# Seven block products in place of eight: the first layer's in-projection of a two-layer decoder trunk, heads 1 to 7

## The chip, the core and the metric

One core of one Trainium2 chip runs the whole program. The metric is the device time of one execution in microseconds (us), lower is better. The core has five engines with an instruction stream each: TensorE (PE) multiplies matrices and transposes, VectorE (DVE) and ScalarE (ACT) work element by element, GpSimd (POOL) does a few small operations and issues those DMAs that add to what is at their destination, and SyncE (SP) issues most of the others. Each works through its own stream in order and waits on semaphores for the others. Matrix products end in PSUM, eight banks of 128 partitions x 512 float32 each; everything else lives in SBUF or, outside the core, in HBM.

## The reference

Two residual layers on 512 tokens of width 2048. Only the first concerns us: RMSNorm, one input projection to queries, keys, values and gate, differential attention with 8 heads, and an output projection.

```python
proj = h @ w_in                                   # (512, 2048) @ (2048, 8192)
q, k, v, gate = jnp.split(proj, 4, axis=-1)
q = q.reshape(B, T, DA_HEADS, 2, DA_HEAD_DIM)     # 8 heads, two halves of 128
v = v.reshape(B, T, DA_HEADS, DA_VALUE_DIM)       # 256 a head
q = apply_rope(rms_norm(q, q_gain), cos, sin)
k = apply_rope(rms_norm(k, k_gain), cos, sin)
...
s = jnp.einsum('bqhcd,bkhcd->bhcqk', qj, k) * scale
p = jax.nn.softmax(jnp.where(mask, s, neg), axis=-1)
a = p[:, :, 0] - lam * p[:, :, 1]
o = jnp.einsum('bhqk,bkhd->bqhd', a, vf)
...
o = rms_norm(o, subln_w) * (1.0 - lambda_init)
return (o * jax.nn.silu(gate)) @ w_out
```

The second layer is RWKV-7 time mixing with projections of its own; the change leaves it alone.

## The kernel before

Every large product is made of three matmuls: each float32 operand is split into a high and a low part, and `mm3` (L127) adds high x high, high x low and low x high. The weights come from HBM in float32: `load_w` (L73) issues the DMA on SP into a tile `wraw` of two K tiles (K is the contracted dimension, 2048 = 16 tiles of 128 rows), and `split_w` (L98) makes `wh` on ACT (L115) and `wl` on DVE (L116). There are three buffers of `wraw` and four each of `wh` and `wl`. The normalised input, transposed, stays in SBUF for the whole layer as `hH` and `hL`, 16 pairs of tiles of 128 rows x 512 tokens.

Per head the layer runs two units, `unit_tok` (L194): first queries and keys, then values and gate. A unit has 512 columns and 512 tokens; it goes through the 16 K tiles, and for each multiplies the four token tiles into the four banks `pp`: 16 x 4 x 3 = 192 matmuls. After the first unit `head_qk` (L297) copies the banks out, applies the rotary tables and the norms; `turn_qk` (L342) transposes the result into `qkT` and `qkL`. After the second, `head_vg` (L353) makes `V`, `VL` and the gate `G` straight from the banks.

The attention of the head before runs inside these units. A `Chain` (L135) is a list of steps; `tick` (L179) counts projection matmuls and puts in the next step when its gap has passed, 40 matmuls for a round of `attention` (L373): scores and softmax of a block of 128 queries, the transposes of `a`, the weighing of `V`, the transposes of `y`. So PE always has projection matmuls between two steps of attention. Two PSUM banks hold scores, one the transposes (tag `pb`), one the weighing. The scheduler writes each engine's stream; work under `high_priority` moves ahead of its place in the program (splits by 2000, steps of a chain by 5000).

The last head's attention runs inside the output projection, with a gap of 21. The output projection already makes half of its columns with seven products (`seven`, L530), on 12 of its 16 K tiles, with sums of weight blocks made by DMAs that add (`add_w`, L524).

Of the kernel before, what the change touches and what calls it, by code (L numbers as in the profile page):

```python
# [296 lines left out]
def head_qk(g, h, qk):  # L297

    nc, w = g.nc, g.work
    sq = g.small.tile([P, NT, 2], F32, name="sq", tag="sq")  # L300
    ss = g.small.tile([P, NT, 4], F32, name="ss", tag="ss")
    rr = g.small.tile([P, NT, 4], F32, name="rr", tag="rr")
    t1s = []
    for t in range(NT):
        t1s.append(w.tile([P, 512], F32, name="t1", tag="t1", bufs=4))
        with g.tc.high_priority(offset=AHEAD):
            nc.scalar.copy(t1s[t][:], qk[t][:])
    for t in range(NT):
        squares = w.tile([P, 512], F32, name="squares", tag="junk", bufs=2)
        t1 = t1s[t]  # L310
        nc.scalar.activation(squares[:], t1[:], AF.Square, scale=g.rstd0[:, t : t + 1])
        t2 = w.tile([P, 512], F32, name="t2", tag="t2", bufs=1)
        t1v = t1[:].rearrange("p (a b c) -> p a b c", a=2, b=2)
        t2v = t2[:].rearrange("p (a b c) -> p a b c", a=2, b=2)

        def tab(x, lo, hi):
            return x[:, t, :, None, lo:hi].to_broadcast([P, 2, 2, hi - lo])

        nc.vector.tensor_mul(t2v[:, :, :, 0:64], t1v[:, :, :, 64:128], tab(g.S, 0, 64))
        nc.vector.tensor_mul(t2v[:, :, :, 64:128], t1v[:, :, :, 0:64], tab(g.S, 64, 128))  # L320
        nc.vector.reduce_sum(ss[:, t, :], squares[:].rearrange("p (c d) -> p c d", c=4), AX.X)
        nc.vector.tensor_mul(t1v, t1v, tab(g.C, 0, P))
        nc.vector.tensor_add(t1[:], t1[:], t2[:])
# [1311 lines left out]
```

## Time and profile before

| | |
|---|---|
| three runs | 2149.81, 2147.76, 2150.05 us; median 2149.81 |
| the profiled execution | 2147.86 us, of which the span of the core 2146.2 us |
| granted TensorE clock | 1.00 of full speed |
| first layer, heads 2 to 6 | 98.6 to 99.0 us each |
| last attention and output projection | about 770 to 1040 us of the span |
| HBM read and written in the span | 207.5 and 16.0 MB |

How to read the lines: a row by stretch gives start and end, the stretch in us, and then the busy time of PE, PE's weight loads, DVE, ACT and POOL, each with its number of instructions, then the granted clock, the DMA engines' busy share and GB/s. A group row gives line, engine, operation, output <- inputs, shapes and count, then busy us and mean ns of one, and after the second bar the idle time ahead of them and what ended it. A timeline row gives start and length in us. Matmuls overlap, so a matmul's length (0.39 us) is more than the time from one start to the next. A DMA row ends in KB each and the median us from issue to landing.

### The profile page before, as it was taken

The page shows a single profiled execution, that of the slowest core. Times are in us where ns is not written, and L with a number is a line of the kernel's source. Part 1 is how long each engine was busy: PE and PEld are TensorE (multiplying, and loading weights), DVE is VectorE, ACT ScalarE, POOL GpSimd, SP SyncE. Part 2 cuts the span into 40 slices and gives each one's busy share as a digit, 9 for nine tenths or more (in the row PEclk, how much of TensorE's full clock was granted, in tenths as well). Part 3 has the DMA queues.
Part 4 walks back from the last instruction along what each step waited for, and adds up shares of the span by engine and source line. Part 5 has one row for each costly group of instructions (what it writes and reads, how often), then busy time and mean ns, then how long its engine had stood idle before and what let it go on. Part 6 is the DMA issues. An engine that isn't in the chain of part 4 may idle for free.

```text
span 2146.2 us, 34955 instructions
## 1 busy us (share of the span) xinstructions
PE 2125.3 (99%) x12260; PEld 1753.2 (82%) x12260; DVE 1547.9 (72%) x4137; ACT 1125.5 (52%) x2587; POOL 339.5 (16%) x614
## 2 busy tenths in 40 slices
PE   9999999999999999999999999999999999999999
PEld 8888888888888887887878888888888888877887
DVE  5665647464656668457789888888888888887645
ACT  6444434343444455445666666666666666666333
POOL 0000000000000000011033233333333223343011
PEclk9999999999999999999999999999999999999999
DMA  6223232322223365672222323222223232345566
GB/s 197 91 82 105 80 99 79 101 97 89 90 87 99 99 196 172 190 152 85 79 69 72 85 77 83 81 77 77 77 77 86 68 81 77 86 125 162 194 168 118
DMA packets 258625, 225.77 MB, mean 105 GB/s; under 512 B 12337, under 2 KB 220481, under 8 KB 258449
## 3 DMA queue, kind: packets, MB, share of 16 engines
q1 hardware_dynamic: 239504, 188.03, 29.5%
q0 software_dynamic: 10080, 19.50, 4.6%
q10 hardware_dynamic: 8864, 16.01, 2.0%
q8 instruction: 96, 1.57, 0.3%
q14 instruction: 81, 0.66, 0.1%
HBM read 207.50 MB, written 15.99 MB: 104 GB/s over the span
## 4 chain that ended last, share of the span: by engine, by line
PE 91%; DVE 5%; ACT 2%; issue 1%; DMA 1%; POOL 0%; ACTq 0%; DVEq 0%; POOLq 0%
PE pp L129 71%; PE pt L129 5%; PE gp L1137 1%; PE o L129 1%; PE sc L129 1%; PE sm L1356 1%; PE sm L1378 1%; PE lora L129 1%; PE sm L1369 1%; DMA yr<-yd 1%; PE Y L1402 1%; DVE wl L116 1%; PE pt L1197 1%; PE pt L346 1%; PE z L129 1%
## 5 line engine op out<-in xcount | busy, mean ns | idle before, releaser
L116 DVE TENSOR_TENSOR wl<-wraw,wh 128x512 fp32r<-128x512 f32 (+1 forms) x636 | 440.4, 694 | 341.3 <-ACT wh L115 335.4
L115 ACT CAST wh<-wraw 128x512 fp32r<-128x512 f32 (+1 forms) x636 | 392.7, 619 | 490.3 <-PE pp L129 387.6
L129 PE MATMUL pp<-wh,hH 128*128 128x512 f32 x1268 | 500.2, 394 | 0.6 <-DVE prmin_rw_mu_dram L234 0.6
L129 PE MATMUL pp<-wh,hL 128*128 128x512 f32 x1268 | 498.1, 393 | 0.0
L129 PE MATMUL pp<-wl,hH 128*128 128x512 f32 x1268 | 497.4, 392 | 0.0
L129 PE MATMUL pp<-hH,wh 128*128 128x512 f32 x1024 | 417.6, 408 | 0.0
L129 PE MATMUL pp<-hL,wh 128*128 128x512 f32 x1024 | 413.2, 404 | 0.0
L129 PE MATMUL pp<-hH,wl 128*128 128x512 f32 x1024 | 413.1, 403 | 0.0
L129 PEld LDWEIGHTS pp<-wh,hL 128*128 128x128 f32 x1268 | 238.4, 188 | 48.6 <-DVE hL L908 0.2
L129 PEld LDWEIGHTS pp<-wh,hH 128*128 128x128 f32 x1268 | 238.4, 188 | 48.3 <-issue 1.3
L129 PEld LDWEIGHTS pp<-wl,hH 128*128 128x128 f32 x1268 | 238.5, 188 | 47.1
L129 PEld LDWEIGHTS pp<-hH,wh 128*128 128x128 f32 x1024 | 193.1, 189 | 38.1 <-issue 1.1
L129 PEld LDWEIGHTS pp<-hH,wl 128*128 128x128 f32 x1024 | 193.4, 189 | 33.3
L129 PEld LDWEIGHTS pp<-hL,wh 128*128 128x128 f32 x1024 | 193.3, 189 | 32.1
L1364 POOL COPY SA<-VS 64x64 f32<-64x64 f32 x224 | 75.2, 336 | 524.8 <-DVE VS L1382 466.2
L1230 DVE SCALAR_TENSOR_TENSOR tmpl<-LT,n,Tm 128x60 f32<-128x60 f32 (+24 forms) x496 | 135.8, 274 | 13.3
L500 POOL DMA_DIRECT2D frow<-yd x12 | 8.9, 742 | 794.6 <-DVE rs_t L67 675.7
L1233 DVE TENSOR_TENSOR Tm<-Tm,tmpl 128x60 f32<-128x60 f32 (+24 forms) x496 | 106.2, 214 | 13.6
L1359 ACT COPY rhs<-sm 64x64 f32<-64x64 f32 x256 | 52.5, 205 | 64.0 <-PE sm L1356 61.1
L1371 ACT COPY VS<-sm 64x64 f32<-64x64 f32 x256 | 52.8, 206 | 55.8 <-PE sm L1369 49.5
L1382 DVE SCALAR_TENSOR_TENSOR VS<-sm,gam,Sg 64x64 f32<-64x64 f32 x192 | 53.9, 281 | 21.7 <-PE sm L1378 16.9
L1356 PEld LDWEIGHTS sm<-VS,G 128*128 128x128 f32 x256 | 47.4, 188 | 17.3 <-PE pp L129 4.3
(339 smaller groups left out, 3284.2 us busy)
## 6 DMA issues: line engine op xcount, KB each, us to landing
wraw<-in_rw_w_in_dram SPq DMA_DIRECT2D x128, 512.0 KB, 4.0
wraw<-in_da_w_in_dram SPq DMA_DIRECT2D x254, 256.0 KB, 3.0
wraw<-in_da_w_out_dram SPq DMA_DIRECT2D x26, 512.0 KB, 4.3
wraw<-in_rw_w_out_dram SPq DMA_DIRECT2D x26, 512.0 KB, 4.3
yr<-yd SPq DMA_DIRECT2D x28, 256.0 KB, 3.4
frow<-yd POOLq DMA_DIRECT2D x12, 512.0 KB, 6.9
xq<-in_x_dram SPq DMA_DIRECT2D x16, 256.0 KB, 5.4
xd<-xq ACTq DMA_DIRECT2D x16, 256.0 KB, 4.1
```

Source lines behind the costliest of these rows:

```text
L115: nc.scalar.copy(hi[:], raw[:, k : k + n])
L116: nc.vector.tensor_sub(lo[:], raw[:, k : k + n], hi[:].bitcast(F32))
L129: m = nc.tensor.matmul(out, a, b, start=s, stop=e, skip_group_check=skip)
L346: nc.tensor.transpose(pt[:, c * P : (c + 1) * P], t1s[t][:, c * P : (c + 1) * P], g.ident[:])
L1137: m = nc.tensor.matmul(gp[h][:, i * P : (i + 1) * P], BK[r_, c0 + i, :, :], p.AR[r_, c0 + i, :, :], start=True, stop=True)
L1230: st = nc.vector.scalar_tensor_tensor(tt, LT[:, i : i + 1, i + 1 :].to_broadcast([P, s, n]), n2[:, i : i + 1], Tm[:, 0:s, i : i + 1].to_br ...
L1233: nc.vector.tensor_add(Tm[:, 0:s, i + 1 :], Tm[:, 0:s, i + 1 :], tt)
L1356: nc.tensor.matmul(sm[:, 0:P], both(p.G[:, c, 0]), both(VS[:, c]), start=True, stop=True)
L1359: rc = nc.scalar.copy(rhs[r_, :], sm[r_, h * C : h * C + C])
L1364: nc.gpsimd.tensor_copy(p.SA[r_, c - 1, :], VS[r_, c, h, :])
L1371: vc = nc.scalar.copy(VS[r_, c, h, :], sm[r_, P : P + C])
L1382: g.state = nc.vector.scalar_tensor_tensor(VS[r_, c + 1, h, :], s_, p.gam[r_, c : c + 1], Sg[r_, :], ALU.mult, ALU.add)
```

## The change

For heads 1 to 7, ten of the sixteen K tiles are taken as two halves of five, the 512 columns of `w_in` stand as two halves of 512 (queries and keys; values and gate), and the tokens as two halves of 256. On these 2 x 2 blocks the product is made with seven block products instead of eight, in the Strassen-Winograd form. The other six K tiles are multiplied as before. What is new in the text:

- `Seven.forms` makes, inside head 0's second unit, the sums of input blocks S1, S2, S4 (their own tiles), and S3 in place of one block of `hH` and `hL`.
- `Seven.head` replaces both units of a head. The four banks are two pairs, B and A, which take turns; results that are needed later go to four SBUF tiles `u` (`U`, `W`) by copies on ACT and sums on DVE (`take`, L646).
- Sums of weight blocks are made in the tile `T` (five K tiles) and, for S1, in `wraw`: a plain DMA of SP, then DMAs of POOL that add. `prime` starts the next head's `T`.
- A split (`Seven.split`) serves two token tiles, 6 matmuls, in the products and 12 in the plain part.
- Room for these tiles comes from the attention, whose `qkT`, `qkL`, `p0`, `p1`, `at`, `al`, `y` have one buffer instead of two; `a` is written over `p0`. The round of attention has a new order and a gap of 37. The squares of `rope` are now four instructions with the sum read from the accumulator, in place of one and a reduction.
- In the output projection the homes of `xq`, of the sums and of loads move to other tiles.

```diff
-            qk = unit_tok(g, g.hH, g.hL, qk_cols(aps, h), 512) if h else qk0
-            t1s, sq = head_qk(g, h, qk)
-            qkT = head_qkT(g)
...
-            vg = unit_tok(g, g.hH, g.hL, [(win, 2 * D + h * 256, 256), (win, 3 * D + h * 256, 256)], 512)
...
+        vg = unit_tok(g, g.hH, g.hL, [(win, 2 * D, 256), (win, 3 * D, 256)], 512, more=u.forms, late=False)
...
+        for h in range(1, NH):
+            Chain(g, attention(g, h - 1, *before, 37), 28)
+            before = u.head(h)
...
+KP = 5
+GROUPS = ((0, 2), (2, 2), (4, 1))
+class Seven:
...
+    def fetch(self, raw, k0, half, h, add=False):
+        n = raw.shape[1]
+        src = self.win[k0 * P : (k0 + n) * P, 2 * half : 2 * half + 2, h, :].rearrange("(k p) f c -> p k f c", p=P)
+        for f in range(2):
+            o, i = raw[:, :, f * 256 : f * 256 + 256], src[:, :, f, :]
+            if add:
+                self.g.nc.gpsimd.dma_start(out=o, in_=i, accum_op=ALU.add)
+            else:
+                self.g.nc.sync.dma_start(out=o, in_=i)
...
+    def mm(self, out, lhs, w, first, end):
+        for t in range(2):
+            mm3(self.g.nc, out[t][:], *lhs(t), w[0][:], w[1][:], first, end, self.g, True)
+    def product(self, out, lhs, h, raw, first, groups=GROUPS, then=None, end=True):
+        for k, n in groups:
+            for i, w in enumerate(self.split(raw(k, n))):
+                kk = k + i
+                self.mm(out, lhs(kk), w, first and kk == 0, end and kk == KP - 1)
+            if then:
+                then(k, n)
+    def plain(self, half, h, outs):
+        for k in range(2 * KP, KT, 2):
+            ws = self.split(self.raw(2, k, half, h))
+            for x, out, first, end in outs:
+                for i, w in enumerate(ws):
+                    self.mm(out, self.rows(k + i, x), w, first and k + i == 2 * KP, end and k + i == KT - 1)
...
+    def head(self, h):
+        q = QK(g)
+        self.product(B, lambda k: self.rows(k, 1), h, tile_of, True, then=more(0, 0))
+        self.product(A, top, h, lambda k, n: self.raw(n, k, 0, h), True)
+        self.copy(W, B)
+        self.product(B, low, h, lambda k, n: self.raw(n, KP + k, 0, h), True, end=False)
+        self.copy(q.t1s[:2], A)
+        self.product(A, lambda k: self.form("S2", k), h, tile_of, False, then=more(KP, 0), end=False)
+        self.copy(U, A)
+        self.plain(0, h, ((0, B, False, True), (1, A, False, False)))
+        self.take(q.t1s[:2], q.t1s[:2], B)
+        self.product(A, lambda k: self.rows(KP + k, 1), h, tile_of, False)
+        if h + 1 < NH:
+            self.prime(h + 1)
+        for t in range(2):
+            rope(g, q, t)
+        self.take(q.t1s[2:], A, W)
+        self.product(B, lambda k: self.form("S1", k), h, lambda k, n: self.raw(n, k, 0, h, (k, 1)), True)
+        for t in range(2, NT):
+            rope(g, q, t)
+        norm_qk(g, q)
+        qkT = head_qkT(g)
+        Chain(g, keys(g, q, qkT, 18), 20)
+        last = lambda k, n: self.raw(n, KP + k, 1, h)
+        s4 = lambda k: self.form("S4", k)
+        self.take(U, B, U, ALU.subtract)
+        self.product(A, s4, h, last, True, GROUPS[:1])
+        self.plain(1, h, ((0, A, False, False), (1, B, True, True)))
+        self.take(W, U, W, ALU.subtract)
+        self.product(A, s4, h, last, False, GROUPS[1:])
+        vg = VG(g)
+        for c in list(g.chains):
+            c.finish(g)
+        self.take(W, W, B)
+        self.take(U, U, A)
+        with g.tc.high_priority(offset=AHEAD if h == NH - 1 else 0):
+            for t, x in ((2, W[0]), (3, W[1]), (0, U[0]), (1, U[1])):
+                vg.convert(g, t, x)
...
     for i in range(NT + 3):
+        if i > 2:
+            turn_y(i - 3)
+        if i == NT + 2:
+            break
+        if 1 < i:
+            weigh(i - 2)
         if 0 < i <= NT:
             turn(i - 1)
-        if i == NT + 2:
-            turn_y(i - 3)
-            break
         yield 8
-        if i > 1:
-            weigh(i - 2)
-        if i > 2:
-            turn_y(i - 3)
         if i < NT:
             scores(i)
         yield gap - 8
```

Three places in the streams. First DVE, early in a head's work on values and gate, where the rotary steps (`t`, `t1`, `t2`) and the norm's small steps (`rs_i`, `rs_t`) of the same head stand among the splits `wl`. Before, in the middle of head 2's second unit, the two splits of a load stand among the same steps, and nothing there reads `pp`:

```order
L64 TENSOR_SCALAR rs_i_2733<-rs_i_2733 128x1
L324 TENSOR_SCALAR ss_2610<-ss_2610 128x16
L322 TENSOR_TENSOR t1_2616<-t1_2616,ropeC_642 128x512
L67 TENSOR_TENSOR rs_t_2734<-rs_i_2733 128x1
L116 TENSOR_TENSOR wl_2800<-wraw_2796,wh_2799 128x512
L68 SCALAR_TENSOR_TENSOR rs_t_2734<-rs_t_2734,so_2729 128x1
L116 TENSOR_TENSOR wl_2804<-wraw_2796,wh_2803 128x512
L70 SCALAR_TENSOR_TENSOR rs_i_2733<-rs_t_2734,rs_i_2733 128x1
L323 TENSOR_TENSOR t1_2616<-t1_2616,t2_2638 128x512
```

Now, in head 2, around the end of the product with S1 (into banks 1242 and 1243; `u` are the four SBUF tiles):

```order
L70 SCALAR_TENSOR_TENSOR ro_2948<-rs_t_2950,rs_i_2949 128x1
L607 TENSOR_TENSOR wl_3133<-wraw_3125,wh_3132 128x512
L454 TENSOR_TENSOR ro_2948<-ro_2948,r_2784 128x1
L324 TENSOR_TENSOR t1_2326<-t1_2326,t2_3079 128x512
L455 SCALAR_TENSOR_TENSOR y_2944<-o_2931,ro_2948,G_2288 128x256
L646 TENSOR_TENSOR u_1246<-pp_1242,u_1246 128x512
L646 TENSOR_TENSOR u_1247<-pp_1243,u_1247 128x512
L646 TENSOR_TENSOR u_1248<-u_1246,u_1248 128x512
L646 TENSOR_TENSOR u_1249<-u_1247,u_1249 128x512
L607 TENSOR_TENSOR wl_3152<-wraw_3148,wh_3151 128x512
L607 TENSOR_TENSOR wl_3156<-wraw_3148,wh_3155 128x512
L607 TENSOR_TENSOR wl_3194<-wraw_3190,wh_3193 128x512
```

Four sums that read the product's banks have come in between the last split of S4's first group (`wl_3133`) and the first split of the plain part (`wl_3152`).

Second PE, in the round of attention with three blocks in flight. Before (head 2's first unit): the transposes of `a` into `pt`, eight projection matmuls, then the weighing into `o`:

```order
L129 MATMUL pp_2147<-wh_2481,hH_462 128x512
L410 MATMUL pt_2501<-ident_79,a_2456 128x128 x3
L129 MATMUL pp_2147<-wl_2482,hH_462 128x512
L129 MATMUL pp_2147<-wh_2481,hL_463 128x512
L129 MATMUL pp_2148<-wh_2481,hH_462 128x512
L129 MATMUL pp_2148<-wl_2482,hH_462 128x512
L129 MATMUL pp_2148<-wh_2481,hL_463 128x512
L129 MATMUL pp_2149<-wh_2481,hH_462 128x512
L129 MATMUL pp_2149<-wl_2482,hH_462 128x512
L129 MATMUL pp_2149<-wh_2481,hL_463 128x512
L129 MATMUL o_2517<-V_2115,at_2385 128x256
```

Now, at the same round (`a` lies in `p0`):

```order
L460 MATMUL yt_2707<-ident_79,y_2588 128x128 x2
L129 MATMUL o_2711<-V_2286,at_2611 128x256
L129 MATMUL o_2711<-VL_2287,at_2611 128x256
L129 MATMUL o_2711<-V_2286,al_2612 128x256
L129 MATMUL o_2711<-V_2286,at_2611 128x256
L129 MATMUL o_2711<-VL_2287,at_2611 128x256
L129 MATMUL o_2711<-V_2286,al_2612 128x256
L436 MATMUL pt_2738<-ident_79,p0_2642 128x128 x3
```

The transposes of `y` and the weighing have moved ahead of the transposes of `a`, without projection matmuls between; `yt` and `pt` are the same bank.

Third POOL, between the constants and the output projection. Before, nothing stands there:

```order
L223 DMA prow_1132<-in_rw_mu_dram 64x128
L971 DMA mut_1134<-in_rw_mu_dram 2x96
L500 DMA frow_8587<-yd_75 128x2x512 x2
L500 DMA frow_8655<-yd_75 128x2x512 x2
L500 DMA frow_8746<-yd_75 128x2x512 x2
L526 DMA ropeC_642<-in_da_w_out_dram 128x2x512
```

Now, one head's share of the adding DMAs: into `wraw` for S1, into the next head's `T`, and twice more into `T` in that head:

```order
L575 DMA wraw_3009<-in_da_w_in_dram 128x2x256 x2
L575 DMA wraw_3034<-in_da_w_in_dram 128x2x256 x2
L575 DMA wraw_3059<-in_da_w_in_dram 128x256 x2
L575 DMA T_715<-in_da_w_in_dram 128x2x256 x4
L575 DMA T_715<-in_da_w_in_dram 128x256 x2
L575 DMA T_715<-in_da_w_in_dram 128x2x256 x4
L575 DMA T_715<-in_da_w_in_dram 128x256 x2
L575 DMA T_715<-in_da_w_in_dram 128x2x256 x4
L575 DMA T_715<-in_da_w_in_dram 128x256 x2
```

These are 24 DMAs that were not there, in a stream that was empty in this part of the program.

More of the change, by code (lines that the diff above doesn't have):

```diff
@@ L294, in lambda_full @@
     nc.vector.tensor_scalar(g.neglam[:], g.neglam[:], LAMBDA_INIT, None, ALU.subtract)
[L297 to L323, printed above, removed]
@@ new lines, with __init__, rope, tab @@
+class QK:
+    def __init__(self, g):
+        self.t1s = [g.work.tile([P, 512], F32, name="t1", tag="t1", bufs=4) for _ in range(NT)]
+        self.sq = g.small.tile([P, NT, 2], F32, name="sq", tag="sq")
+        self.ss = g.small.tile([P, NT, 4], F32, name="ss", tag="ss", bufs=2)
+        self.rr = g.small.tile([P, NT, 4], F32, name="rr", tag="rr", bufs=2)
+def rope(g, q, t):
+    nc, t1 = g.nc, q.t1s[t]
+    t2 = g.work.tile([P, 512], F32, name="t2", tag="t2", bufs=1)
+    for c in range(4):
+        cs = slice(c * P, (c + 1) * P)
+        nc.scalar.activation(t2[:, cs], t1[:, cs], AF.Square, scale=g.rstd0[:, t : t + 1],
+                             accum_out=q.ss[:, t, c : c + 1])
+    t1v = t1[:].rearrange("p (a b c) -> p a b c", a=2, b=2)
+    t2v = t2[:].rearrange("p (a b c) -> p a b c", a=2, b=2)
+    def tab(x, lo, hi):
+        return x[:, t, :, None, lo:hi].to_broadcast([P, 2, 2, hi - lo])
+    nc.vector.tensor_mul(t2v[:, :, :, 0:64], t1v[:, :, :, 64:128], tab(g.S, 0, 64))
+    nc.vector.tensor_mul(t2v[:, :, :, 64:128], t1v[:, :, :, 0:64], tab(g.S, 64, 128))
+    nc.vector.tensor_mul(t1v, t1v, tab(g.C, 0, P))
+    nc.vector.tensor_add(t1[:], t1[:], t2[:])
@@ L377, in attention @@
+def attention(g, h, qkT, qkL, sq, vg, gap, rows=None):
+    nc, w = g.nc, g.work
+    V, VL, G = vg.V, vg.VL, vg.G
     yT = w.tile([P, 2, T], F32, name="yTh", tag="yTh", bufs=1)
@@ L513, in sum_forms @@
         else:
-            at = [pool.tile([P, n, 256], F32R, name="f" + nm, tag=t, bufs=m)[:] for pool, t, m in tags]
+            at = [x[0].tile([P, n, 256], F32R, name="f" + nm, tag=x[1], bufs=x[2])[:] if type(x) is tuple else x
+                  for x in tags]
         out[nm] = []
@@ L759, in new_x @@
         def new_x(cb):
-            xq = g.work.tile([P, NT, 512], F32, name="xq", tag=("qkT", "qkL")[cb // 2], bufs=2)
+            w = g.work
+            if cb < 2:
+                xq = w.tile([P, NT, 512], F32, name="xq", tag=("qkT", "qkL")[cb], bufs=1)
+            elif cb == 2:
+                xq = Tokens([w.tile([P, 512], F32, name="xq", tag="t1", bufs=4) for _ in range(NT)])
+            else:
+                both = [w.tile([P, 2, 512], F32, name="xq", tag=t, bufs=1) for t in ("VL", "V")]
+                xq = Tokens([x[:, i] for x in both for i in range(2)])
             for t in range(NT):
```

218 lines of the change are left out of this document (154 added, 64 removed).

## The prediction

> **What bounds the kernel now.** I read the engine shares first, then the chain of work that ended last, then the stretches of two whole heads, and last what the matmul engine waited for.
>
> ```profile
> span 2146.2 us, 34955 instructions
> PE 2125.3 (99%) x12260; PEld 1753.2 (82%) x12260; DVE 1547.9 (72%) x4137; ACT 1125.5 (52%) x2587; POOL 339.5 (16%) x614
> PE 91%; DVE 5%; ACT 2%; issue 1%; DMA 1%; POOL 0%; ACTq 0%; DVEq 0%; POOLq 0%
> 574.55 18.17 PE pp L129 x80
> 475.60:574.30 98.70, 98.70 (x474) 82.31 (x473) 57.68 (x179) 41.56 (x92) 0.00 (x0) 1.00 0.28 91
> 574.30:673.00 98.70, 98.70 (x474) 82.31 (x473) 57.73 (x179) 41.56 (x92) 0.00 (x0) 1.00 0.29 91
> PE pt L410 <- DVE a L404: 2.1, 3, 1.7
> ```
>
> The reader is to see four things. TensorE (PE) is busy for 99% of the span, and the chain lies on it for 91%. A stretch of the chain inside a head is 80 projection matmuls in 18.17 us, so one 128x512 matmul costs 18.17 / 80 = 0.2271 us from start to start. The two rows by stretch are heads of the first layer: 98.70 us, PE busy in all of it, granted clock 1.00, while VectorE (DVE) works 57.7 us, ScalarE (ACT) 41.6 us, GpSimd (POOL) nothing, and HBM gives 91 GB/s at a DMA share of 0.28. And the largest wait of PE in this layer, for the softmax row `a`, is 2.1 us in all. So in these heads time is the number of PE instructions times their interval; every matmul that goes takes its interval with it, as long as nothing else becomes late.
>
> **The change, part by part.**
>
> *Removed: matmuls.* Per head and before, 2 units x 16 K tiles x 4 token tiles x 3 (the split into high and low parts) = 384 projection matmuls. Afterwards: seven products x 5 K tiles x 2 x 3 = 210, and 6 plain K tiles x 2 column halves x 4 x 3 = 144, together 354. That is 30 fewer in each of 7 heads: 210 x 0.2271 = **-47.7 us**. Of 384 x 0.2271 = 87.2 us, 11.5 us of a 98.7 us head are attention and transposes; they stay, so a head should take 91.9 us.
>
> *Added: weight splits, sums and copies on DVE and ACT.* They lie beside PE and cost only what they make late.
>
> ```profile
> L115 ACT CAST wh<-wraw 128x512 fp32r<-128x512 f32 x32 | 19.9, 624 | 39.1 <-PE pp L129 38.3 <-ACT p L396 0.5
> L116 DVE TENSOR_TENSOR wl<-wraw,wh 128x512 fp32r<-128x512 f32 x33 | 22.6, 690 | 34.2 <-ACT wh L115 34.2
> L307 ACT COPY t<-pp 128x512 f32<-128x512 f32 x4 | 2.3, 598 | 0.0
> L311 ACT ACTIVATE squares<-t,rstd 128x512 f32<-128x512 f32 x4 | 2.7, 745 | 0.0
> L321 DVE TENSOR_REDUCE ss<-squares 128x4 f32<-128x512 f32 x4 | 2.7, 681 | 0.0
> L323 DVE TENSOR_TENSOR t<-t,t 128x512 f32<-128x512 f32 x4 | 2.7, 685 | 0.0
> L396 ACT ACTIVATE p<-sc,nb,sq 128x128 f32<-128x128 f32 x2 | 0.9, 452 | 1.3 <-DVE nb L393 1.3
> L396 ACT ACTIVATION_READ_ACCUMULATOR p<-sc,nb,sq 128x1 f32 x8 | 1.6, 194 | 0.0
> ```
>
> A head splits 7 x 5 + 2 x 6 = 47 weight tiles instead of 32. DVE: 15 x 0.690 = 10.4, twelve block sums at the 0.685 of such an addition = 8.2, minus four reductions at 0.681 = 2.7: 57.7 + 15.9 = 73.6 us in 91.9 us, 80%. ACT: 15 x 0.624 = 9.4, two more copies at 0.598 = 1.2, sixteen 128-wide squares with their read of the accumulator, (0.452 + 0.194) x 16 = 10.3, minus four wide squares at 0.745 = 3.0: 41.6 + 17.9 = 59.5 us, 65%. Neither becomes the bound by its sum. But DVE works strictly in the order written, and now block sums that wait for PE stand in front of splits that PE waits for.
>
> *The tightest such place* is the four sums (`u`) after the fourth column block's product S1, shown under the change. Starts on DVE are closer than durations. One row is by duration
>
> ```profile
> L430 DVE SCALAR_TENSOR_TENSOR y<-o,ro,G 128x256 f32<-128x256 f32 x4 | 1.9, 482 | 0.1
> ```
>
> and the order of starts:
>
> ```profile
> 561.39 0.42 DVE L320 TENSOR_TENSOR t<-t,ropeS 128x256 f32<-128x256 f32 x1
> 561.72 0.15 DVE L70 SCALAR_TENSOR_TENSOR rs_i<-rs_t,rs_i 128x1 f32<-128x1 f32 x1
> 561.79 0.68 DVE L116 TENSOR_TENSOR wl<-wraw,wh 128x512 fp32r<-128x512 f32 x1
> 562.39 0.15 DVE L67 TENSOR_TENSOR rs_t<-rs_i 128x1 f32<-128x1 f32 x1
> 562.47 0.68 DVE L322 TENSOR_TENSOR t<-t,ropeC 128x512 f32<-128x512 f32 x1
> 563.07 0.15 DVE L68 SCALAR_TENSOR_TENSOR rs_t<-rs_t,so 128x1 f32<-128x1 f32 x1
> 563.14 0.16 DVE L64 TENSOR_SCALAR rs_i<-rs_i 128x16 int32<-128x16 int32 x1
> ```
>
> A full-width operation holds DVE 0.60 us (561.79 to 562.39), a half-width one 0.33, a small one 0.07; `y` by the same cut of 0.08 about 0.40. From the end of the product before S1, DVE has eight full-width, ten small, two half-width operations and `y` to do, about 6.9 us by such intervals; then the four sums, 2.4, then the split for the first plain tile, 0.6, and some 0.3 to learn that PE is done: 10.2 us. PE has 30 + 12 matmuls, two transposes and one matmul more before it needs that split: 43 x 0.2271 + 0.2 = 10.0 us. So 0.2 us late by intervals; with the full durations in place of intervals (eight times 0.69, ten times 0.16 and so on, 11.9 us in all with the sums and the split) 2.2 us late; zero if DVE is early. I take 0.5 x 7 = **+3.5 us** (0 to 15.4), nearer to the intervals, because those are what the rows show. The same count at the change of heads (takes of W and U, then V, gs, G and the next splits) leaves DVE about 0.9 us ahead of PE; no cost, and its bound is within the 15.4.
>
> *Attention in one buffer each, and its new order.* The transposes of `y`, the weighing and the transposes of `a` now stand together, and the first and the last share one PSUM bank. So the transposes of `a` wait until ACT has copied `yT` out.
>
> ```profile
> 566.42 0.28 PE L129 MATMUL o<-VL,at 128*128 128x256 f32 x1
> 566.54 0.28 PE L129 MATMUL o<-V,al 128*128 128x256 f32 x1
> 566.66 0.38 PE L435 MATMUL yt<-ident,y 128*128 128x128 f32 x2
> 566.80 0.48 PE L129 MATMUL pp<-wh,hL 128*128 128x512 f32 x1
> 574.17 0.38 PE L435 MATMUL yt<-ident,y 128*128 128x128 f32 x2
> 574.59 0.37 ACT L436 COPY yTh<-yt 128x256 f32<-128x256 f32 x1 [0.46 <-PE yt L435]
> ```
>
> The copy starts 0.42 us after the transposes did and takes 0.37: 0.79 us. Between lie two transposes (566.66 to 566.80, 0.14 us) and six weighing matmuls at 0.12 us: 0.86 us in one block of a head, 1.2 in the next. Free ACT: no wait. A split of 0.62 us in front of the copy: 0.56 and 0.2 us. I take 0.2 for each of 8 attentions, **+1.6 us** (0 to 6.4). The matmuls between scores and transposes of `a` fall from 32 to 29, a loss of 0.7 us of slack; single buffers of p, at and al are each read, in PE's order, before they are written again. No cost.
>
> *Loads and adding DMAs.* A head reads 37 weight tiles by SP and 20 by POOL's adding DMAs instead of 32 by SP: 57 x 0.262 MB = 14.9 MB in 91.9 us, with the stores 168 GB/s.
>
> ```profile
> 900.00:925.00 25.00, 25.00 (x112) 20.73 (x111) 12.64 (x19) 11.16 (x21) 3.56 (x3) 1.00 0.70 187
> wraw<-in_da_w_in_dram SPq DMA_DIRECT2D x254, 256.0 KB, 3.0
> wraw<-in_da_w_out_dram SPq DMA_DIRECT2D x26, 512.0 KB, 4.3
> T<-in_rw_w_out_dram POOLq DMA_DIRECT2D x3, 512.0 KB, 8.5
> q0 software_dynamic: 10080, 19.50, 4.6%
> ```
>
> From 900 to 925 us the output projection already runs a product of this kind, 6 matmuls a split and sums added by DMA, at 187 GB/s and a share of 0.70, with PE busy throughout; its loads of 512 KB land in 4.3 us. The three load buffers hold 5 K tiles, which last 5 x 6 x 0.2271 = 6.8 us; a load may start when its buffer was split, so landing, cast and split (0.62 + 0.69) must fit into 6.8: up to 5.5 us for the landing, against 3.0 to 4.3. The sums in `T` have a product or more between write and read (at least two products, 13.6 us, against a longest landing of 8.5). DMA share: 0.28 x 37 / 32 for SP's part, over a head of 91.9 instead of 98.7, is 0.35; POOL's 5.24 MB at its queue's 19.50 MB in 4.6% of 2146.2 is 26.5 us of all engines, 0.29; sum 0.64. If packets of half the length took as long each, 0.93. I take 0.64, nearest to the measured 0.70, and no cost; the other end is a rival.
>
> *Elsewhere.* Head 0's second unit makes the sums S1, S2, S4: some 60 half-width operations on DVE, 60 x 0.33 = 20 us, in a stretch where DVE is now idle for 44 - 26.5 = 17.5 us:
>
> ```profile
> 55.70:99.70 44.00, 44.00 (x203) 36.46 (x202) 26.52 (x67) 19.23 (x36) 4.66 (x9) 1.00 0.31 98
> 770.00:841.00 71.00, 68.42 (x335) 56.15 (x333) 47.73 (x147) 35.13 (x78) 1.44 (x2) 1.00 0.56 180
> ```
>
> So DVE has hardly any room there, but its splits may run up to four tiles ahead: +1 us (0 to 5). The last attention, at its short gap, loses PE 71.00 - 68.42 = 2.58 us today; it keeps the gap and loses double buffers, and I leave it (-2.6 to +2.6). Output projection and second layer keep their instructions; only homes of buffers differ.
>
> *The sum:* -47.7 + 3.5 + 1.6 + 1 = -41.6. Against the profiled execution's own 2147.86 us (its span and 1.7 us around it) this is **2106.3 us**. The median of the three runs, 2149.81, lies 1.95 above that execution.
>
> *A rule of the skill, weighed.* The rows first:
>
> ```profile
> 901.95 0.69 DVE L116 TENSOR_TENSOR wl<-T,wh 128x512 fp32r<-128x512 f32 x1 [0.66 <-ACT wh L115]
> 902.95 1.19 POOL L526 DMA_DIRECT2D T<-in_da_w_out_dram  x1 [0.97 <-DVE wl L116]
> 903.32 0.69 DVE L116 TENSOR_TENSOR wl<-wraw,wh 128x512 fp32r<-128x512 f32 x1 [0.67 <-ACT wh L115]
> ```
>
> While POOL issues an adding DMA (902.95 to 904.14) DVE starts and ends a split, at its usual 0.69 us. The Trainium skill, "SBUF — State Buffer", section "SBUF: two separate sides", says that DVE and GpSimd share one pair of ports under an exclusive lock, that whichever starts first keeps it for its whole instruction, and that an operation with two SBUF inputs (a split is one) is kept out by a GpSimd operation that reads SBUF. This trace does not show such a block for a DMA's issue; what it would cost is the third rival.
>
> **The rivals.**
>
> *DVE late (faster, but less).* If at both tight places DVE runs by its full durations, 2.2 us a head at the sums and as much again at the change of heads: 31 us in place of 3.5, 2134 us; at one place alone 2118. For it: DVE at 80%, strictly in order, with no spare at the sums. Against: the interval rows, and the stretch 900 to 925, where the same 6 matmuls a split, with DVE at 12.64 / 25 = 51%, left PE no gap.
>
> *Loads late (slower than before).* Place: two products in a row that load their tiles, and the S4 and plain groups behind S1. Were the landing of a pair 8.5 us, the longest adding row, a buffer's turn takes 8.5 + 1.3 = 9.8 instead of 6.8: 3 us for each of some three such places and for the S1 group that is loaded and then added to, four in all, 12 a head, 84 in 7 heads: 2190 us. It decides from 5.5 us on, and turns the sign once a head loses 41.6 / 7 = 5.9 us, 1.5 at each place, at a landing of 7.0. For it: a share up to 0.93 by half-length packets. Against: 4.3 us at a share of 0.70.
>
> *POOL's issues hold DVE up (slower).* 24 issues a head x 1.19 = 28.6 us; DVE would need 73.6 + 28.6 = 102.2 us for a head of 98.7: 3.5 x 7 = +24.5, 2172 us. It decides above (98.7 - 73.6) / 24 = 1.05 us an issue. Against: the last rows quoted.
>
> That the change does not do what it says is out: in the built programs 7092 matmuls write `pp` before and 6882 after, 210 fewer.
>
> **How the numbers follow.** Forecast (stalls of up to some 12 us beside the saving) 0.77; DVE late 0.13; loads late 0.04; POOL holding DVE 0.02; the rest, a wait that I have not found that eats all of it, 0.04, half of it within 0.2%. A measurement of this kernel can tell about 0.2%, 4.3 us, from no change. Faster 0.77 + 0.13 + 0.01 = 0.91, same 0.03, slower 0.06. The range: below, no stalls and no loss in the last attention, 2147.9 - 47.7 - 2.6 = 2097.6; above, all upper bounds, 2106.3 + 11.9 + 4.8 + 4 + 2.6 = 2129.6, which takes in DVE late at one place. 2098 to 2129.
>
> **What would show it.** Right: a head of 91.9 us by the spacing of `yt` or of the first scores, PE busy in all but 1 us of it, DVE near 74 and ACT near 60 us a head, DMA share near 0.64 at 168 GB/s, PE's waits on `wl` in the first layer near 0.5 us a head. DVE late: PE idle 2 us or more a head behind `u` or `VL`. Loads late: casts of `wraw` waiting for SP's DMAs, landings beyond 5.5 us. POOL: splits beyond 0.7 us during issues. Wrong altogether: a head of 98 us or more.

## The result and the profile after

| | before | after |
|---|---|---|
| median of four runs of each | 2149.93 us | 2117.28 us |
| lowest and highest | 2147.76, 2151.22 | 2115.37, 2119.22 |
| the profiled execution, its span | 2147.86, 2146.2 | 2117.56, 2115.9 |
| last matmul of the output projection starts at | 979.00 | 946.63 |

The ratio after / before is 0.9849, 95% interval 0.9832 to 0.9866: the kernel became faster by 32.65 us. The forecast was 2106.3 us, 41.6 us faster than the profiled execution; the time lies 11 us above that and inside the stated range of 2098 to 2129. (The table of the time before gives about 1040 us as the end of the output projection; by the trace its last matmul starts at 979.00 and the second layer's first at 982.21.)

First the shares of the engines on the page of the changed kernel, then its stretches of two whole heads (columns as before).

```profile
PE 2088.3 (99%) x12050; PEld 1714.9 (81%) x12050; DVE 1656.3 (78%) x4352; ACT 1228.7 (58%) x2948; POOL 525.1 (25%) x782
291.69:384.53 92.84, 92.76 (x444) 76.56 (x443) 70.83 (x201) 54.90 (x137) 26.50 (x24) 1.00 0.73 167
384.53:479.91 95.38, 93.88 (x444) 76.30 (x443) 71.35 (x203) 54.84 (x138) 26.47 (x24) 1.00 0.71 163
```

PE has exactly the 210 instructions less that were counted (12260 - 12050). A head takes 92.84 us at best, where 91.9 were forecast; and two heads of the same program, with the same instructions, differ by 2.5 us. DVE has 71 us in a head (73.6 forecast), ACT 55 (59.5), HBM gives 163 to 167 GB/s (168), and the DMA share is 0.71 to 0.73 (0.64).

The waits of PE in the changed kernel (us in total, times, longest us), those of the first layer:

```profile
PE yt L460 <- DVE y L455: 3.0, 5, 1.4
PE pt L370 <- ACT t L337: 2.7, 4, 1.3
...
PE pt L436 <- DVE p L430: 1.3, 2, 0.9
...
PE yt L460 <- DVE rs_t L67: 1.1, 1, 1.1
...
PE pp L129 <- DVE gs L392: 0.8, 1, 0.8
...
PE pp L129 <- DVE wl L116: 0.3, 1, 0.3
...
PE pp L129 <- DVE wl L607: 0.2, 1, 0.2
```

The split `wl` of these heads (L607), on which the forecast put its stall, is waited for once, 0.2 us. PE waits for `y` and for the scaled keys `t` instead. All waits of PE up to the last matmul of the output projection are 10.7 us, against 3.9 before (sums over the timeline of PE, without the 1.9 us at the program's start).

What makes `t` late is seen where the slow head and a quick one reach the first plain tile behind the product with S1. The timeline of ACT, the quick head first, then the slow one; the idle time and its cause stand in brackets:

```profile
360.03 0.62 ACT L606 CAST wh<-wraw 128x512 fp32r<-128x512 f32 x1 [0.65 <-PE pp L129]
363.05 0.62 ACT L606 CAST wh<-wraw 128x512 fp32r<-128x512 f32 x1 [2.40 <-DMA wraw<-in_da_w_in_dram]
...
453.30 0.62 ACT L606 CAST wh<-wraw 128x512 fp32r<-128x512 f32 x1 [0.66 <-PE pp L129]
458.67 0.62 ACT L606 CAST wh<-wraw 128x512 fp32r<-128x512 f32 x1 [4.75 <-DVE u L646]
```

The cast reads `wraw` alone; the sums `u` named in the second head have nothing to give it. In the quick head the same cast waits for its DMA, and in the slow one it does too: the load issued at 451.66 landed after 6.9 us, at 458.57, and the cast started at 458.67. The landing times of SP's loads in a stretch of 30 us around these casts, first the quick head, then the slow one:

```profile
DMA to landing us min/median/max: 2.8/4.0/4.9
```

```profile
DMA to landing us min/median/max: 2.7/4.2/7.1
```

In the slow head the longest load took 7.1 us; the forecast's own limit was 5.5. Behind these loads the four splits, the rotary steps and the norm stand in DVE's stream, and PE stops at the transposes of the keys:

```profile
467.42 0.39 PE L129 MATMUL pp<-wh,hL 128*128 128x512 f32 x1
469.08 0.33 PE L370 MATMUL pt<-ident,t 128*128 128x128 f32 x1 [1.27 <-ACT t L337]
```

Two theories follow. **Loads:** the adding DMAs make plain loads land late now and then, and DVE, with no slack, passes it on. **DVE:** its stream itself, with the sums `u` in it, is too long at this place.

### The profile page after: what moved, and what is told of

Same layout as the page of the kernel before. It is cut to its first block, busy times and chain, and to the rows that moved or that the text cites. A ratio compares the mean times of both kernels' runs of the same rounds, so it can differ in the third digit from the quotient of the medians.

```text
span 2115.9 us, 35878 instructions
## 1 busy us (share of the span) xinstructions
PE 2088.3 (99%) x12050; PEld 1714.9 (81%) x12050; DVE 1656.3 (78%) x4352; ACT 1228.7 (58%) x2948; POOL 525.1 (25%) x782
## 3 DMA queue, kind: packets, MB, share of 16 engines
q0 software_dynamic: 48608, 56.21, 16.4%
## 4 chain that ended last, share of the span: by engine, by line
PE 61%; DVE 5%; ACT 2%; issue 1%; DMA 0%; POOL 0%; ACTq 0%; DVEq 0%; POOLq 0%
PE pp L129 44%; PE pt L129 5%; PE gp L1347 1%; PE sm L1566 1%; PE sm L1588 1%; PE lora L129 1%; PE sm L1579 1%; PE Y L1612 1%; DVE wl L116 1%; PE pt L1407 1%; PE z L129 1%; DMA yr<-yd 0%; PE px L1474 0%; PE Y L1616 0%; DVE tmpl L1440 0%
## 5 line engine op out<-in xcount | busy, mean ns | idle before, releaser
L129 PE MATMUL pp<-wh,hL 128*128 128x512 f32 x988 | 389.3, 394 | 0.0
L129 PE MATMUL pp<-wh,hH 128*128 128x512 f32 x988 | 387.9, 394 | 0.9 <-DVE gs L392 0.8
L129 PE MATMUL pp<-wl,hH 128*128 128x512 f32 x988 | 387.8, 393 | 0.6 <-DVE wl L116 0.3
L115 ACT CAST wh<-wraw 128x512 fp32r<-128x512 f32 (+1 forms) x412 | 253.7, 617 | 201.1 <-PE pp L129 111.0
L116 DVE TENSOR_TENSOR wl<-wraw,wh 128x512 fp32r<-128x512 f32 (+1 forms) x412 | 286.8, 697 | 106.4 <-ACT wh L115 101.9
L575 POOL DMA_DIRECT2D T<-in_da_w_in_dram x126 | 139.5, 1674 | 364.1 <-DVE wl L607 193.4
L606 ACT CAST wh<-wraw 128x512 fp32r<-128x512 f32 x224 | 137.7, 620 | 129.0 <-PE pp L129 71.6
L607 DVE TENSOR_TENSOR wl<-wraw,wh 128x512 fp32r<-128x512 f32 x224 | 152.6, 689 | 50.9 <-ACT wh L606 47.9
L1440 DVE SCALAR_TENSOR_TENSOR tmpl<-LT,n,Tm 128x60 f32<-128x60 f32 (+24 forms) x496 | 135.8, 274 | 13.3
L129 PE MATMUL pp<-wh,S 128*128 128x512 f32 x420 | 136.9, 396 | 0.0
L129 PEld LDWEIGHTS pp<-wh,S 128*128 128x128 f32 x420 | 78.8, 188 | 17.6
```

The costliest lines, as they stand in the source:

```text
L115: nc.scalar.copy(hi[:], raw[:, k : k + n])
L116: nc.vector.tensor_sub(lo[:], raw[:, k : k + n], hi[:].bitcast(F32))
L129: m = nc.tensor.matmul(out, a, b, start=s, stop=e, skip_group_check=skip)
L575: self.g.nc.gpsimd.dma_start(out=o, in_=i, accum_op=ALU.add)
L606: g.nc.scalar.copy(hi[:], raw[:, k])
L607: g.nc.vector.tensor_sub(lo[:], raw[:, k], hi[:].bitcast(F32))
```

## The experiments

All start from the changed kernel. Times are medians of four runs. They vary by 2 us and more from run to run for a reason that the last section gives in part, and the kernel before, run beside each of the four batches of runs, had medians of 2149.68 (e1 to e4), 2149.48 (e5 to e8), 2147.82 (e9 to e11) and 2148.23 us (e12). So what concerns the first layer is read from the trace: the start of the last matmul of the output projection (946.63 us in the changed kernel), and the spacing from one attention's last transposes of `y` to the next one's, of four heads. Each of these is from one execution, and the last stage alone makes 1 us of difference between e1 and e5, so differences of 1.5 us and less settle nothing. PE's waits are counted as above, from a matmul's modelled end, 0.39 us after its start; by starts each is some 0.16 us longer (0.39 - 0.23), and shorter ones are not in the sum. The table is followed by the runs.

| run | median us | last matmul us | spacing of four heads, us | PE's waits until then, us |
|---|---|---|---|---|
| before | 2149.93 | 979.00 | 98.74 to 98.79 | 3.9 |
| changed kernel | 2117.28 | 946.63 | 92.90 to 95.01 | 10.7 |
| e1, no adding DMAs | 2109.84 | 940.95 | 92.87 to 92.89 | 6.2 |
| e2, no sums `u` | 2112.85 | 943.42 | 92.89 to 93.42 | 8.6 |
| e3, rows in place of S | 2112.16 | 946.48 | 92.57 to 93.96 | 13.3 |
| e4, keys later | 2113.71 | 946.05 | 92.98 to 94.39 | 11.0 |
| e5, no adds into T | 2109.79 | 939.68 | 92.83 to 92.89 | 6.1 |
| e6, no adds for S1 | 2114.77 | 945.11 | 92.88 to 93.61 | 9.7 |
| e7, next T later | 2116.17 | 947.87 | 92.91 to 94.04 | 11.2 |
| e8, `y` later | 2115.79 | 945.46 | 93.31 to 95.01 | 10.1 |
| e9, plain writes into T | 2111.72 | 941.27 | 92.87 to 93.75 | 7.3 |
| e10, S in planes | 2114.99 | 946.87 | 92.97 to 94.11 | 11.4 |
| e11, W on POOL | 2116.75 | 950.26 | 93.29 to 95.30 | 14.2 |
| e12, e5 and e2 together | 2110.13 | 939.72 | 92.82 to 92.92 | 5.5 |

**e1 to e4: which of the two, and two smaller things.** e1:

```diff
             if add:
-                self.g.nc.gpsimd.dma_start(out=o, in_=i, accum_op=ALU.add)
-            else:
-                self.g.nc.sync.dma_start(out=o, in_=i)
+                continue
+            self.g.nc.sync.dma_start(out=o, in_=i)
```

> The 24 adding DMAs of each head are left out, so the weight sums are wrong; everything else stays. In the changed kernel heads 3 to 6 take 92.8, 95.4, 93.1 and 94.3 us, and in the slow ones PE waits up to 1.3 us for the scaled keys (t) behind a weight load. Theory 'loads': the adding DMAs make the plain loads behind the product with S1 land late; without them all four heads take about 92.8 us, PE's waits for t vanish, the kernel gains 4 to 6 us (2111 to 2113). Theory 'DVE': the four sums u and the rotary steps stand in DVE's stream and make t late; nothing changes, heads still differ by 2 us, time within 2 us of 2117.

A head of e1, in the columns of the stretches above:

```profile
267.40:360.20 92.80, 92.72 (x443) 76.59 (x442) 71.06 (x202) 55.47 (x137) 0.00 (x0) 1.00 0.34 111
```

DVE and ACT have the same work as before the edit; POOL has none, and the DMA share is 0.34 instead of 0.73. All four heads take 92.9 us, the waits for `t` in heads 1 to 7 are gone, and the median is 7.4 us lower, more than the 4 to 6 expected. Theory "loads" holds. The waits for `y` in heads 1 and 2 went too.

e2:

```diff
-        self.take(U, B, U, ALU.subtract)
...
-        self.take(W, U, W, ALU.subtract)
```

> The four sums U = B - U and W = U - W behind the product with S1 are left out, so values and gate are wrong. It takes 2.4 us of DVE work from the tightest place of each head. Theory 'DVE': PE's waits for t (2.1 us in heads 4 to 6, and 2.6 with what is hidden in modelled ends) go, 2113 to 2115. Theory 'loads': the cast behind the sums still waits for its DMA, t is at most as much earlier as the sums were in its way, the waits of PE for t in the slow heads stay at over half, 2116 to 2118. By the forecast's own term, priced at 0.5 us a head, 3.5 us would go.

The layer ends 3.2 us earlier, and waits for `t` of 0.2 and 1.2 us and one for `y` of 0.8 us stay. Taken alone this is the forecast's term of 3.5 us, and it would have passed for a proof of "DVE"; e12 shows that it is not.

e3:

```diff
     def form(self, n, k):
-        return lambda t: [self.S[n][:, k, i, t * P : t * P + P] for i in range(2)]
+        return self.rows(KP + k if n == "S4" else k, 1)
```

> The products with S1, S2 and S4 read their stationary rows from hH and hL instead of from the sum tiles (same sizes, wrong products; the sums are still formed in head 0). In the changed kernel a matmul with S starts 0.2327 us after the one before, one with hH or hL 0.2279. Theory 'operand': it is the tile that is slower; the 630 matmuls go at 0.228 and 3 us go, 2114. Theory 'place': it is where they stand (two banks in turn, DMA and DVE traffic at that moment); the matmuls at these places still take 0.233, no change, 2117.

The timeline of PE at the same place, first the changed kernel, then e3 (start, length; "x2" is two matmuls):

```profile
357.91 0.40 PE L129 MATMUL pp<-wl,S 128*128 128x512 f32 x1
358.14 0.63 PE L129 MATMUL pp<-wh,S 128*128 128x512 f32 x2
358.61 0.40 PE L129 MATMUL pp<-wl,S 128*128 128x512 f32 x1
358.84 0.63 PE L129 MATMUL pp<-wh,S 128*128 128x512 f32 x2
359.31 0.40 PE L129 MATMUL pp<-wl,S 128*128 128x512 f32 x1
```

```profile
355.14 0.39 PE L129 MATMUL pp<-wh,hH 128*128 128x512 f32 x1
355.36 0.39 PE L129 MATMUL pp<-wl,hH 128*128 128x512 f32 x1
355.59 0.39 PE L129 MATMUL pp<-wh,hL 128*128 128x512 f32 x1
...
356.50 0.39 PE L129 MATMUL pp<-wh,hH 128*128 128x512 f32 x1
```

Six matmuls with S take 359.31 - 357.91 = 1.40 us, 0.233 each; six with hH and hL 356.50 - 355.14 = 1.36, 0.227 each. So it is the operand and not the place. The layer's end hardly moved, though: in this execution the granted clock stood at 0.66 from 765 to 770 us of the span, which costs 5 x 0.34 = 1.7 us (without that the end would be near 944.8), and PE's waits are 2.6 us longer.

e4:

```diff
-        Chain(g, keys(g, q, qkT, 18), 20)
+        Chain(g, keys(g, q, qkT, 16), 28)
```

> The chain that transposes queries and keys starts 28 projection matmuls after its place instead of 20, with 16 instead of 18 between its four steps; nothing else. Eight matmuls are 1.8 us, more than the longest wait for t (1.43 us with what is hidden in modelled ends). Both theories: the waits for t go in heads 4 to 6, 2.6 us in all, waits for y (yt) stay, 2114 to 2115. If what makes t late is shifted along, or the end of the head waits for the transposes, nothing is gained: 2117.

A miss by the trace: waits for `t` of 1.26 and 1.07 us stand in two heads, and the layer ends 0.6 us earlier. The median of 2113.71 is 3.6 us below that of the changed kernel, and all four runs are below its lowest; but in the profiled executions the second layer, which has the same instructions in both, makes 3.3 us of difference (949.63 to 2108.22 us, 1158.6, against 1161.9), so the runs don't show that the edit brought it. A late load isn't a fixed distance that eight matmuls could bridge.

**e5 and e6: which adding DMAs.** e5 leaves out the adds in `prime` and in `add` (18 of a head's 24, those into `T`), e6 those in `raw`, in this order:

```diff
-            for k, n in GROUPS:
-                self.fetch(self.T[:, k : k + n], k, 1, h, add=True)
...
-            self.fetch(self.T[:, k : k + n], k0 + k, half, h, add=True)
+            pass
```

```diff
-            if also:
-                self.fetch(raw, *also, h, add=True)
```

> The 18 adding DMAs of each head into T are left out, the 6 into wraw (for S1) stay; weight sums are wrong. Without all 24 the last matmul of the output projection started at 940.95 us of the span instead of 946.63, the waits of PE up to there fell from 10.7 to 6.2 us, loads of 256 KB landed in 2.9 us instead of 3.8, and heads 3 to 6 took 92.9 us each. Theory 'traffic': adding DMAs share the DMA engines with the plain loads and lengthen their landing, each about alike; 18 of 24 bring at least 4 us, last matmul near 942, landing near 3.1. Theory 'turn': what costs is that a buffer of wraw is held for a load and then an add, one after the other, in the group for S1; then little is gained, last matmul after 945.

> The opposite half: the 6 adding DMAs of each head into wraw are left out, the 18 into T stay; the weight sums for S1 are wrong. Theory 'traffic': a quarter of the 5.7 us, last matmul of the output projection near 945, loads still land in 3.6 to 3.8 us. Theory 'turn': most of the 5.7 us, last matmul at 941 to 943, heads 3 to 6 alike.

The adds into `T` carry most of it: 7.0 us by the layer's end, the adds for S1 1.5 us. "Traffic" holds against "turn". The shares don't add up to those of e1, which leaves out both and ends 5.7 us earlier. Ahead of the output projection, at the last transposes of `y` inside head 7, the changed kernel stands at 738.67 us, e5 at 731.95, e1 at 732.23 and e6 at 735.82: 6.7, 6.4 and 2.9 us earlier. So each half alone takes away time that the other would have taken as well, and e1 loses its last 1 us behind that point, at a wait of 1.50 us for a split (L116) where e5 waits 0.29.

**e7 and e8: moving things out of the way**, e7 first.

```diff
-        if h + 1 < NH:
-            self.prime(h + 1)
...
         self.product(A, s4, h, last, True, GROUPS[:1])
+        if h + 1 < NH:
+            self.prime(h + 1)
```

```diff
-        yield gap - 8
+        yield gap - 8 + (3 if i == NT + 1 else 0)
```

> The six plain loads and six adding DMAs that start the next head's T move from ahead of the product with S1 to behind the first group of S4; the computation is the reference's. There the plain part follows, which takes a split only every 12 matmuls, and 90 matmuls (20 us) are left before T is needed. Theory 'traffic': the loads of S1, S4 and the first plain tile no longer share the engines with them; PE's waits for t and most of the uneven heads go, last matmul of the output projection at 943 to 945, 2113 to 2115. Theory 'turn': no change, 946 to 947, 2117. If T comes late for the next head instead, PE waits for casts of T at a head's start and it is slower than 2117.

> Three more projection matmuls stand before the last transposes of y of each attention; nothing else. In the changed kernel seven heads lose 0.25 us there (and heads 1 and 2 lose 1.2 and 1.6), because DVE finishes y after PE gets to its transposes. Three matmuls are 0.68 us: 0.25 x 5 and twice 0.68, 2.6 us, go, last matmul of the output projection at 944, 2114 to 2115. If y is late because DVE as a whole runs behind PE there, DVE's other results are late instead and it stays at 2117.

Both fell short of what was expected. In e7 the waits for `t` are 0.25, 0.47, 0.50 and 1.29 us: the adds collide with other loads instead. (The clock stood at 0.66 from 185 to 190 us here as well, 1.7 us; without it the end is near 946.2, no change.) In e8 the waits for `y` in heads 1 and 2 fell from 1.06 and 1.41 to 0.32 and nothing, but PE now waits for `t` in five heads, 0.28 to 1.07 us. Some 0.24 us ahead of the last transposes of `y` stayed in most heads of every run, three matmuls later too, so a wait for `y` is unlikely; what it is stays open. It isn't the operand S either, as in e3, without S, it is 0.45.

**e9: what in an adding DMA costs.** The same DMAs into `T`, same bytes and queue, without the addition:

```diff
-                self.g.nc.gpsimd.dma_start(out=o, in_=i, accum_op=ALU.add)
+                acc = dict(accum_op=ALU.add) if raw.shape[0] and add == 2 else {}
+                self.g.nc.gpsimd.dma_start(out=o, in_=i, **acc)
...
-                self.fetch(raw, *also, h, add=True)
+                self.fetch(raw, *also, h, add=2)
```

> The 18 DMAs of a head that add into T are issued by POOL as before, with the same source, size and place, but write instead of adding; the weight sums in T are wrong. Theory 'bytes': it is the bytes read and their queue that slow the plain loads; landing stays at 3.8 us, heads stay uneven (93 to 95 us), last matmul of the output projection 945 to 947. Theory 'adding': a DMA that adds holds the engines longer than its bytes say, because it reads its destination too; landing falls to 3.0 to 3.3 us and most of the 7 us that came when these DMAs were left out comes here too, last matmul at 940 to 942.

POOL's queue (packets, MB, share of 16 engines) and the DMA groups (KB each, median us to landing) of the changed kernel, of e5 and of e9:

```profile
q0 software_dynamic: 48608, 56.21, 16.4%
wraw<-in_da_w_in_dram SPq DMA_DIRECT2D x226, 256.0 KB, 3.8
T<-in_da_w_in_dram POOLq DMA_DIRECT2D x84, 256.0 KB, 5.4
```

```profile
q0 software_dynamic: 19712, 28.68, 7.6%
wraw<-in_da_w_in_dram SPq DMA_DIRECT2D x226, 256.0 KB, 3.0
```

```profile
q0 software_dynamic: 28448, 56.21, 11.7%
wraw<-in_da_w_in_dram SPq DMA_DIRECT2D x226, 256.0 KB, 3.0
T<-in_da_w_in_dram POOLq DMA_DIRECT2D x84, 256.0 KB, 3.1
```

The 27.5 MB into `T` (56.21 - 28.68) are 8736 packets as plain writes and 28896 as adds, take 4.1% of the engines as the one and 8.8% as the other, and land in 3.1 against 5.4 us. With plain writes SP's loads land in 3.0 us as if there were no traffic into `T` at all, and 5.4 of the 7.0 us are back. So it is the adding, not the bytes; the other 1.6 us are near what single executions differ by. Whether an add costs more because its packets are a third as long (953 bytes against 3151) or because it must read what is there, e9 does not separate.

**e10 and e11: two repairs that keep the computation**, e10 first.

```diff
-        self.S = {n: g.work.tile([P, KP, 2, 256], F32R, name=n, tag=n, bufs=1) for n in ("S1", "S2", "S4")}
+        self.S = {n: g.work.tile([P, 2, KP, 256], F32R, name=n, tag=n, bufs=1) for n in ("S1", "S2", "S4")}
...
-        return lambda t: [self.S[n][:, k, i, t * P : t * P + P] for i in range(2)]
+        return lambda t: [self.S[n][:, i, k, t * P : t * P + P] for i in range(2)]
```

```diff
-        self.take(W, U, W, ALU.subtract)
+        for w, u in zip(W, U):
+            g.nc.gpsimd.tensor_tensor(out=w[:], in0=u[:], in1=w[:], op=ALU.subtract)
```

> The sum tiles S1, S2, S4 hold all high parts and then all low parts (2 x 5 x 256) instead of high and low by turns (5 x 2 x 256); the computation is the reference's. With stationary rows from hH and hL in place of these tiles the 630 matmuls went from 0.233 to 0.228 us. Theory 'layout': high and low next to each other in one tile make the difference; the interval falls to 0.228, 3 us, 2114. Theory 'tile': one tile for both, in whatever order, or where it lies; 0.233 and 2117 stay.

> The two sums W = U - W behind the product with S1 are made by POOL instead of DVE; they read and write SBUF alone; the computation is the reference's. DVE has 1.2 us less to do at its tightest place. Theory 'slack' (late loads cost PE time only because DVE has no slack behind them): half of the 3.2 us that leaving out all four sums brought, last matmul of the output projection at 945, 2115 to 2116. Theory 'shared port' (DVE and GpSimd keep each other out of SBUF): POOL's sums take longer than 1.2 us and hold up DVE's splits beside them, nothing gained or slower, 2117 to 2125.

e10: the 573 starts of one matmul with S right behind another are 0.233 us apart as in the changed kernel; not the order of high and low parts. (One of its four runs took 2123.5 us; the others lie between 2114.0 and 2115.1.)

e11 ended the layer 3.6 us later by its trace. Its median of 2116.75 doesn't show it, with runs from 2112.2 to 2120.1; the rows do show what the sums on POOL did to DVE. First the timeline of POOL and then of DVE in e11, and last the same place of DVE in the changed kernel:

```profile
365.03 3.00 POOL L682 TENSOR_TENSOR u<-u 128x512 f32<-128x512 f32 x2 [5.91 <-DVE u L646]
```

```profile
365.45 4.32 DVE L607 TENSOR_TENSOR wl<-wraw,wh 128x512 fp32r<-128x512 f32 x4
```

```profile
365.22 2.50 DVE L607 TENSOR_TENSOR wl<-wraw,wh 128x512 fp32r<-128x512 f32 x4
```

Four splits take 4.32 us beside two sums on POOL, and 2.50 us without them. A single split's time (min/median/max in ns) in the changed kernel and in e11:

```profile
L607 DVE TENSOR_TENSOR wl<-wraw,wh x224: 678/691/696, 112.6 to 760.1; 128x512 fp32r<-128x512 f32 x112
```

```profile
L607 DVE TENSOR_TENSOR wl<-wraw,wh x224: 678/691/1834, 112.5 to 763.7; 128x512 fp32r<-128x512 f32 x112
```

So POOL's sums keep DVE's splits out, and POOL's 168 adding DMAs never did: no split was over 0.696 us beside them, nor any of the 105 splits of `T`. The Trainium skill, "SBUF — State Buffer", section "SBUF: two separate sides", states an exclusive lock between DVE and GpSimd, and e11's 1.834 us agree with it; in the changed kernel's row no issue of a DMA on POOL held a split up.

**e12: do the sums `u` cost anything by themselves?** The edits of e5 and e2 together.

> Both are left out: the 18 adding DMAs of a head into T, and the four sums u behind the product with S1 (weight sums, values and gate are wrong). Alone they brought the last matmul of the output projection from 946.63 us to 939.68 and 943.42. Theory 'slack': the sums cost PE nothing as long as the loads are in time, they only leave DVE no room to make up for a late one; heads stay at 92.9 us, last matmul at 939 to 940. Theory 'two costs': each has its own price, 7.0 and 3.2 add up; heads at 92.4, last matmul near 936.5.

939.72 against 939.68 us: the sums cost nothing while the loads are in time. The 7.0 and 3.2 us are the same time, once at its source and once at the place where DVE could have made up for it. "Slack" holds.

## Why the prediction came out as it did

The direction and the bound were right, and three quarters of the size came: PE bounds these heads before and after, and its instructions less are the gain. By the steps of the sum:

| step | forecast us | measured us |
|---|---|---|
| removed matmuls, 7 heads | -47.7 | -41.3 (e5) |
| four sums `u` late | +3.5 | 0 (e12) |
| transposes of `a` behind `yT` | +1.6 | 0 as waits |
| head 0 | +1 | +0.8 |
| loads and adding DMAs | 0 | +7.0 (e5) |
| last attention | 0 (-2.6 to +2.6) | +0.4 |
| sum | -41.6 | -33.1 |

To the end of the output projection the trace has 946.63 - 979.00 = -32.4, the medians -32.65; 0.7 us of the sum are not accounted for. That the total came as near is in part luck: 5.1 us of the forecast's cost (3.5 and 1.6) stood for things that cost nothing, and without them the forecast would have been -46.7.

*Removed matmuls, mis-sized.* A head without late loads takes 92.86 us (e5), against 98.76 before: (98.76 - 92.86) x 7 = 41.3. The 30 matmuls went with their interval, but what stayed became dearer by 0.96 us a head (92.86 instead of 91.9). 90 matmuls of a head now have S as an operand and are 0.2329 us apart (mean of 573 starts) instead of 0.2280 (2021 starts with hH and hL, up to 770 us): 0.44. The weighing stands right behind the transposes of `y` now:

```profile
445.13 0.38 PE L460 MATMUL yt<-ident,y 128*128 128x128 f32 x2
445.27 0.36 PE L129 MATMUL o<-V,at 128*128 128x256 f32 x1
445.47 0.28 PE L129 MATMUL o<-VL,at 128*128 128x256 f32 x1
445.59 0.29 PE L129 MATMUL o<-V,al 128*128 128x256 f32 x1
```

Behind its first matmul the next one starts after 0.20 us (445.27 to 445.47) and not after 0.12 (445.47 to 445.59). The 30 weighing matmuls of a head take 3.84 us instead of 3.55, 0.29. That delay isn't new in itself: before, the projection matmul behind these transposes had its successor after 0.31 us instead of 0.23. But the other groups of a head's matmuls (scores, transposes, projection with hH and hL) changed by 0.1 us or less each, and by nearly nothing together. And 0.24 us stand ahead of the last transposes of `y`. The step took one interval for all matmuls.

*Loads: the step that failed.* It said "I take 0.64, nearest to the measured 0.70, and no cost". That it is the landing that decides, and from about 5.5 us on, agrees with the trace: of the 246 loads of `w_in` by SP in heads 1 to 7 (112 to 755 us) 24 took longer, up to 7.4 us; before, none of 208 did (longest 4.7). But not each of them costs something: in e5 five took longer, up to 6.6, and PE waited for nothing behind them. The DMA share that the step rested on came from the bytes of a queue that held other DMAs. SP's part is 0.34 (a head of e1), as forecast at 0.35; POOL's is 0.73 - 0.34 = 0.39 and not 0.29, since a DMA that adds takes the engines 2.1 times as long as one that writes (8.8% / 4.1%). The rival "loads late" named the mechanism, and priced it as if four places of every head were late, 84 us; now and then one is, 7.0 us in all.

*The sums `u`.* The place was the tightest of DVE, as the forecast had it, but with loads in time DVE gets there early enough: in e5, with the sums in place, PE never waits for a split of these heads, and e12, without them, is no faster. The forecast's own intervals say so too, since its count doesn't give the 6.9 us that it states: 8 x 0.60 + 10 x 0.07 + 2 x 0.33 + 0.40 = 6.6, and so 9.9 us to the split against PE's 10.0, not late. The +3.5 stood close to e2's 3.2 by accident.

*Transposes of `a`.* No wait there in heads 1 to 7; what the new order costs, if anything, is on the weighing, at most 0.29 x 7 = 2.0 us, counted above.

*ACT, 59.5 us forecast and 55 measured.* It bounds nothing; most of the difference is a price: a 128-wide square and its read of the accumulator were priced by durations, 0.65 us, and in the changed kernel the next square starts 0.40 us after the one before (363.57 and 363.97).

*Head 0 and last attention.* PE's waits between 55 and 115 us are 0.61 and 0.81 us, before 0.64; PE is idle for 3.0 us in the last attention, before 2.6.

*POOL's issues hold DVE up.* Out, by the row of e11's section. *DVE late* at full durations: out, DVE's 71 us in a head leave PE without a listed wait in heads 1 to 7 of e1, e5 and e12.

Of the versions that compute what the reference does, e4 has the lowest median; that it is better than the changed kernel isn't shown, for the reason given with e4.

## What to carry to other kernels

Price a DMA that adds by its own rows and not by bytes: here it took the engines 2.1 times as long as a plain one and made the neighbours' loads land 0.8 us later in the median and now and then much later (24 of 246 took over 5.5 us). Where leaving out one of two suspects brings time, leave out both as well: the sums `u` looked like 3.2 us and were only the slack that hid late loads. And when instructions are taken away from a bound engine, count what the order and the operands of the remaining ones do to their intervals.
